# A decoder layer: pool history fetched in the head, pool products moved back, gate columns in fp32, output scaled in pieces

## The chip, the core and the metric

The kernel runs on one core of a Trainium2 chip. The metric is the device time of one execution in microseconds (us). TensorE (PE) multiplies matrices, VectorE (DVE) and ScalarE (ACT) do elementwise work, GpSimd (POOL) does a little elementwise work and issues DMAs, SyncE (SP) only issues DMAs.

## What is computed

One layer of a decoder trunk for 256 prompt tokens and 8 x 8 sample tokens: T = 320 token columns, model width 2048. All tensors are fp32.

```python
mod = silu(c) @ w_ada + b_ada                       # per sequence: sh1 sc1 g1 sh2 sc2 g2
h = rmsnorm(x, norm1_g) * (1 + sc1) + sh1
q, k, v, og, u, ga, gb, alr = split(h @ w_in)       # alr: 16 columns, the gate columns
loga = log_sigmoid(alr @ w_a2 + b_a) / 16
o, s_new = gla(q / 16, k, v, loga, state_gla)       # 4 heads, dk 256, dv 512
y_a = rmsnorm(o, gla_norm_g) * silu(og)
u_ext = concat(state_pool, u)                       # 15 history rows, then the new rows
y_b = (window_mean(u_ext, (2, 4, 8, 16)[g]) - u) @ w_pool[g] * pool_scale
x = x + g1 * ((sigmoid(ga) * y_a + sigmoid(gb) * y_b) @ w_o)
x = x + g2 * (swiglu(rmsnorm(x, norm2_g) * (1 + sc2) + sh2))
y = rmsnorm(x, final_norm_g)                        # also out: new GLA states, last 15 rows of u
```

## The kernel before

Activations lie transposed: features on 128 partitions, 320 tokens along the free axis. A product with a weight is done in three fp32r products (`mm3`): the weight and the activation are each split into a high part (a cast on ACT, `whi`, L157) and a low rest (a subtraction on DVE, `wlo`, L158), and high x high, high x low and low x high are summed in PSUM. Weights come through SP's queue into `raw` tiles of 512 KB; `whi` and `wlo` have four buffers each. A unit of 256 output columns over all 2048 inputs is 96 products into one tile `ps` of the PSUM pool `pmain`, which has two buffers. A unit's result is moved out by ACT or DVE, and only then is its buffer free.

The stages. The head (up to about 250 us) computes `mod` and h slice by slice, and with each slice of h the part that it adds to all units of group 0 (`SLICES`); 4 groups are the 4 heads with their pooling group. In the last slice, behind q's part, `alr_proj` makes the gate columns. Then groups 1 to 3 run: units q, k, v (two), u, og, ga, gb. While group h multiplies, the steps of group h - 1 (`gla_steps`, `pool_steps`, `merge_step`) are taken from a list `queue` ten at a time (`pump`), and a scheduler places all instructions on the engines by its own estimate of times. On the chip each engine then runs its instructions in that order. The tiles q, k, v and u have one buffer for all groups, so q of group 1 can leave PSUM only when the steps of group 0 have read q of group 0. The steps of the gates: `s_gk` (alr times w_a2, L591, then absolute value, exponential and logarithm, L599 to L606), `s_exp` (products with cumulative-sum matrices, L617 and L618, then exponentials, L622 to L627), `s_prod` (products with q and k, L633 to L653, among them kdA, a tile of the w4 buffers, L653), transposes, state products with S (L786, L807), and outputs. `pool_steps`: load history (`s_sp`), put it ahead of u (`s_hist`), write the new history (`s_buf`), window differences (`s_win`, giving dh and dl), and the products with w_pool (`s_y`, tiles `psy`, two PSUM buffers at once). The scaling of w_ada (`ada_burst`, L301) is done in fp32 with 32 columns of weights, four such products side by side in column tiles of TensorE.

After that come w_o, the feed-forward part and, at the end, the final norm: for each block k of 128 features the residual, its square, a transpose into token rows `yn` (L1093 to L1099), then the row sums (L1107), the scale `rr`, and the scaled rows stored through SP (L1119 to L1123).

Of the kernel before, what the change touches and what calls it, by code (L numbers as in the profile page):

```python
# [79 lines left out]
def body(tc, A):  # L80
# [759 lines left out]
    def pool_steps(g):  # L840
        h = g.h
        E = {}
        st = []
        u = g.u

        def s_sp():
            E["sp"] = lp.tile([NB * PB, 256], F32, tag="sp", name=nm("sp"))
            nc.gpsimd.dma_start(E["sp"], A["state_pool"][0, :, :, 256 * h:256 * h + 256].rearrange("b r c -> (b r) c"))
        st.append(s_sp)

        def s_hist():
            G.memset(u[:, :, 0:PB], 0.0)
            _, us = u_parts(g)
            pt = misc()
            for f in range(2):
                tr(pt[:, f * P:f * P + NB * PB], E["sp"][:, f * P:(f + 1) * P])
            for f in range(2):
                V.tensor_copy(us[:, f, :, 0:PB], pt[:, f * P:f * P + NB * PB].rearrange("p (b r) -> p b r", r=PB))
        st.append(s_hist)

        def s_buf():
            _, us = u_parts(g)
            cmt = w4([P, 2, P])
            G.memset(cmt[:, :, TS + PB:], 0.0)
            for f in range(2):
                G.tensor_copy(s3(cmt[:, f, 0:TS]), us[:, f, :, PB:])
                G.tensor_copy(cmt[:, f, TS:TS + PB], u[:, f, UEP - PB:UEP])
            pt = misc()
            for f in range(2):
                tr(pt[:, f * P:(f + 1) * P], cmt[:, f])  # L870
            t = lp.tile([P, DV], F32, tag="sf", name=nm("nb"))[:, 0:256]
            V.tensor_copy(t, pt[:, 0:256])
            for b in range(NB):
                nc.gpsimd.dma_start(A["o_ps"][0, b, PB - LS:PB, 256 * h:256 * h + 256], t[8 * b:8 * b + 8])
            nc.gpsimd.dma_start(A["o_pp"][0, 0, :, 256 * h:256 * h + 256], t[TS:TS + PB])
        st.append(s_buf)

        def s_win():
            cur = u
            ws = 1  # L880
            n = 0
            while ws < WINDOWS[h]:
                t = w4([P, 2, UEW])
                V.tensor_tensor(t[:, :, ws:], cur[:, :, ws:], cur[:, :, 0:UEW - ws], op=ALU.add)
                if 2 * ws < WINDOWS[h]:
                    V.tensor_copy(t[:, :, 0:ws], cur[:, :, 0:ws])
                cur = t
                ws *= 2
            w = WINDOWS[h]
            d = w4([P, 2, T])  # L890
            up, us = u_parts(g)
            cp_, cs = cur[:, :, PB:UEP], cur[:, :, UEP:UEW].rearrange("p f (b t) -> p f b t", t=PB + LS)
            V.scalar_tensor_tensor(d[:, :, 0:TP], cp_, 1.0 / w, up, op0=ALU.mult, op1=ALU.subtract)
            for f in range(2):
                V.scalar_tensor_tensor(s3(d[:, f, TP:T]), cs[:, f, :, PB:], 1.0 / w, us[:, f, :, PB:],
                                       op0=ALU.mult, op1=ALU.subtract)
                V.tensor_tensor(d[:, f, 0:16], cp_[:, f, 0:16], invc[:, 16 * h:16 * h + 16], op=ALU.mult)
                V.tensor_tensor(d[:, f, 0:16], d[:, f, 0:16], up[:, f, 0:16], op=ALU.subtract)
            dh = lp.tile([P, 2, T], F32R, tag="dh", name=nm("dh"))
            dl = lp.tile([P, 2, T], F32R, tag="dl", name=nm("dl"))  # L900
            hilo(dh, dl, d)
            E["dh"], E["dl"] = dh, dl
        st.append(s_win)

        def s_y():
            pp = [pmain.tile([P, 2, 512], F32, tag="pm", name=nm("psy")) for _ in range(2)]
            for k, whi, wlo in split_chunk(A["w_pool"][0, h].rearrange("(k p) n -> p k n", p=P), 2, 512):
                for e in range(4):
                    mm3(pp[e // 2][:, e % 2, :T], whi[:, e * P:(e + 1) * P], wlo[:, e * P:(e + 1) * P],
                        E["dh"][:, k], E["dl"][:, k], k == 0, k == 1)  # L910
            for i, ps in enumerate(pp):
                for e in range(2):
                    ee = 2 * i + e
                    V.scalar_tensor_tensor(g.gb[:, ee], ps[:, e, 0:T], PSC[:, 4 * h + ee:4 * h + ee + 1], g.gb[:, ee],
                                           op0=ALU.mult, op1=ALU.mult)
        return st, [s_y]

# [135 lines left out]
    for pi, (f0, f1) in enumerate(parts):  # L1053
# [24 lines left out]
        else:  # L1078
# [4 lines left out]
            for xg in xgs:  # L1083
                G.memset(xg[:, T:3 * P], 0.0)
        for ui in range(8):
            ps = proj(wdn, 256 * ui, f0, f1, ah, al)
            for i in range(2):
                k = 2 * ui + i
                residual(ps, i, k, 5)
                if pi == 1:  # L1090
# [2 lines left out]
                    S.activation(xg[:, 0:T], x1[k], AF.Copy, scale=FG[:, k:k + 1])  # L1093
                    pt = misc()
                    for a in range(3):
                        tr(pt[:, a * P:(a + 1) * P], xg[:, a * P:(a + 1) * P])
                    for a in range(3):
                        n = P if a < 2 else TS
                        (S.copy if a == 0 else V.tensor_copy)(yn[a][:n, k * P:(k + 1) * P], pt[:n, a * P:(a + 1) * P])  # L1099
# [14 lines left out]
    for a in range(3):  # L1114
        n = P if a < 2 else TS
        for c in range(2):
            sl = yn[a][:n, c * 1024:(c + 1) * 1024]
            if c == 0:
                V.tensor_scalar(sl, sl, rr[:n, 2 * a:2 * a + 1], None, op0=ALU.mult)  # L1119
            else:  # L1120
                S.activation(sl, sl, AF.Copy, scale=rr[:n, 2 * a:2 * a + 1])
            dst = A["y_p"][0, a * P:(a + 1) * P] if a < 2 else ys
            nc.sync.dma_start(dst[:, c * 1024:(c + 1) * 1024], sl)  # L1123
# [22 lines left out]
```

## Time and profile before

| | |
|---|---|
| median of 3 runs | 1978.41 us (1978.18 to 1979.74) |
| the profiled execution | 1972.99 us, its span 1971.2 us |
| TensorE busy | 1924.5 us, 98% |
| VectorE, ScalarE, GpSimd busy | 1007.0, 826.9, 207.3 us |
| DMA | 400.60 MB, mean 203 GB/s |
| granted TensorE clock, mean | 0.993 of full |

A row of the timeline gives the start, the time from the first start to the last end of a run of like instructions, the engine, the line of the kernel, the operation, the tiles out<-in, their shapes and how many; in brackets stands how long the engine stood idle ahead of it and what it waited for. Two TensorE instructions overlap, so the step from one start to the next is what one costs. PEld is the weight load, which runs beside the products. The granted clock is 1.00 at full speed and 0.50 at half.

### The profile page before, as it was taken

The page shows a single profiled execution, that of the slowest core. Times are in us where ns is not written, and L with a number is a line of the kernel's source. Part 1 is how long each engine was busy: PE and PEld are TensorE (multiplying, and loading weights), DVE is VectorE, ACT ScalarE, POOL GpSimd, SP SyncE. Part 2 cuts the span into 40 slices and gives each one's busy share as a digit, 9 for nine tenths or more (in the row PEclk, how much of TensorE's full clock was granted, in tenths as well). Part 3 has the DMA queues.
Part 4 walks back from the last instruction along what each step waited for, and adds up shares of the span by engine and source line. Part 5 has one row for each costly group of instructions (what it writes and reads, how often), then busy time and mean ns, then how long its engine had stood idle before and what let it go on. Part 6 is the DMA issues. An engine that isn't in the chain of part 4 may idle for free.

```text
span 1971.2 us, 34613 instructions
## 1 busy us (share of the span) xinstructions
PE 1924.5 (98%) x13808; PEld 1825.2 (93%) x13808; DVE 1007.0 (51%) x1935; ACT 826.9 (42%) x1485; POOL 207.3 (11%) x323
## 2 busy tenths in 40 slices
PE   5999999999999999999999999999999999999997
PEld 4889888988998899989989999999999999999997
DVE  3776454666355535665574444444444444444554
ACT  4433343544345433553354333333333434344443
POOL 2231131221121112111030000000000000000000
PEclk9999989999999999999999999999999999999998
DMA  9996647777875788579845555444545444444442
GB/s 349 354 354 237 203 150 264 219 230 251 256 223 188 247 268 272 183 249 321 269 153 158 186 188 182 145 150 144 156 145 155 150 150 150 150 151 144 149 139 98
DMA packets 287308, 400.60 MB, mean 203 GB/s; under 512 B 11953, under 2 KB 243921, under 8 KB 286809
## 3 DMA queue, kind: packets, MB, share of 16 engines
q1 hardware_dynamic: 250170, 261.81, 42.7%
q0 software_dynamic: 36976, 136.57, 19.5%
q8 instruction: 108, 1.77, 0.4%
q14 instruction: 54, 0.44, 0.1%
HBM read 373.90 MB, written 24.67 MB: 202 GB/s over the span
## 4 chain that ended last, share of the span: by engine, by line
PE 82%; DMA 3%; ACT 1%; DVE 0%; issue 0%; POOL 0%; ACTq 0%; DVEq 0%
PE ps L172 25%; PE ps L171 25%; PE ps L173 25%; PE pm L301 3%; PE pm L135 1%; DMA araw<-w_ada 1%; PE pm L786 1%; PE pm L807 1%; DMA raw<-w_o 1%; DMA S<-state_gla 1%; PE pm L752 1%; DMA o_gs<-S 0%; PE pm L782 0%; PE pm L591 0%; PE pm L741 0%; PE psy L171 0%
## 5 line engine op out<-in xcount | busy, mean ns | idle before, releaser
L158 DVE TENSOR_TENSOR wlo<-raw,whi 128x512 fp32r<-128x512 f32 x952 | 657.7, 694 | 792.4 <-ACT whi L157 779.9
L157 ACT CAST whi<-raw 128x512 fp32r<-128x512 f32 x952 | 587.8, 622 | 948.3 <-PE ps L172 830.1
L171 PE MATMUL ps<-hh,whi 128*128 128x320 f32 x1408 | 441.9, 314 | 6.1 <-ACT hh L337 2.6
L172 PE MATMUL ps<-hl,whi 128*128 128x320 f32 x1408 | 440.4, 313 | 0.0
L173 PE MATMUL ps<-hh,wlo 128*128 128x320 f32 x1408 | 437.4, 312 | 0.0
L172 PE MATMUL ps<-h2l,whi 128*128 128x320 f32 x1408 | 434.7, 309 | 0.0
L171 PE MATMUL ps<-h2h,whi 128*128 128x320 f32 x1408 | 434.7, 309 | 0.0
L173 PE MATMUL ps<-h2h,wlo 128*128 128x320 f32 x1408 | 434.2, 309 | 0.0
L171 PEld LDWEIGHTS ps<-hh,whi 128*128 128x128 f32 x1408 | 265.2, 188 | 19.7 <-issue 9.0
L172 PEld LDWEIGHTS ps<-hl,whi 128*128 128x128 f32 x1408 | 265.3, 188 | 10.4 <-issue 9.4
L173 PEld LDWEIGHTS ps<-hh,wlo 128*128 128x128 f32 x1408 | 264.7, 188 | 8.0 <-issue 5.3
L171 PEld LDWEIGHTS ps<-h2h,whi 128*128 128x128 f32 x1408 | 264.4, 188 | 3.4 <-ACT ah L337 3.4
L172 PEld LDWEIGHTS ps<-h2l,whi 128*128 128x128 f32 x1408 | 264.5, 188 | 0.1
L173 PEld LDWEIGHTS ps<-h2h,wlo 128*128 128x128 f32 x1408 | 264.5, 188 | 0.0
L171 PE MATMUL ps<-ah,whi 128*128 128x320 f32 x704 | 217.7, 309 | 0.0
L172 PE MATMUL ps<-al,whi 128*128 128x320 f32 x704 | 216.5, 308 | 0.0
L173 PE MATMUL ps<-ah,wlo 128*128 128x320 f32 x704 | 216.5, 308 | 0.0
L172 PEld LDWEIGHTS ps<-al,whi 128*128 128x128 f32 x704 | 132.0, 187 | 0.0
L171 PEld LDWEIGHTS ps<-ah,whi 128*128 128x128 f32 x704 | 131.9, 187 | 0.0
L173 PEld LDWEIGHTS ps<-ah,wlo 128*128 128x128 f32 x704 | 131.9, 187 | 0.0
L269 POOL DMA_DIRECT2D araw<-w_ada x64 | 55.1, 864 | 397.2 <-PE pm L301 385.9
L172 PE MATMUL ps<-ml,whi 128*128 128x320 f32 x256 | 79.3, 310 | 0.0
(282 smaller groups left out, 1634.2 us busy)
## 6 DMA issues: line engine op xcount, KB each, us to landing
raw<-w_gu SPq DMA_DIRECT2D x176, 512.0 KB, 3.5
raw<-w_in SPq DMA_DIRECT2D x170, 512.0 KB, 4.4
araw<-w_ada POOLq DMA_DIRECT2D x64, 1024.0 KB, 8.7
raw<-w_down SPq DMA_DIRECT2D x80, 512.0 KB, 3.5
hraw<-w_ada POOLq DMA_DIRECT2D x28, 1024.0 KB, 9.8
S<-state_gla POOLq DMA_DIRECT2D x16, 1024.0 KB, 8.3
o_gs<-S POOLq DMA_DIRECT2D x16, 1024.0 KB, 6.9
raw<-w_o SPq DMA_DIRECT2D x32, 512.0 KB, 6.2
```

What stands on the lines that cost most here:

```text
L135: PE.transpose(out, in_, ident[:k, :k])
L157: S.copy(hi, raw)
L158: V.tensor_sub(lo, raw, hi.bitcast(F32))
L171: PE.matmul(ps, lhsT=whi, rhs=xhi, start=start, stop=False)
L172: PE.matmul(ps, lhsT=whi, rhs=xlo, start=False, stop=False)
L173: last_mm[:] = [PE.matmul(ps, lhsT=wlo, rhs=xhi, start=False, stop=stop).ins]
L269: nc.gpsimd.dma_start(t[:, r:r + step], wada[:, k0 + r:k0 + r + step, col:col + nb * P])
L301: PE.matmul(ps[32 * j:32 * j + 32, 0:w], lhsT=scT[:, k0 + r + j, :], rhs=ada_raw[n][:, r + j, :], start=k0 == 0 and first, stop=k0 + nk == ...
L752: PE.matmul(pt, lhsT=E["kdn"][:, s, d * P:(d + 1) * P], rhs=E["vn"][:, s], start=s == 0, stop=s == 1)
L786: PE.matmul(pt[32 * j:32 * j + 32, :], lhsT=qeP[:, d, 4 * gg + j, :], rhs=E["S0", gg, d][:, j], start=False, stop=d == 0, tile_position=(0 ...
L807: PE.matmul(pt, lhsT=E["kpn"][:, j, d * P:(d + 1) * P], rhs=E["vp"][:, gg], start=True, stop=True)
```

## The change

Four things are done.

- The gate columns: `alr_proj` no longer splits the 16 columns of w_in into high and low parts in `wal` tiles. It multiplies the fp32 columns (`walr`, padded to 32) with hh and with hl, both read as fp32, in four column tiles; each tile sums a quarter of the input blocks. The four partial sums lie in four strips of 32 rows of alr, and w_a2 is loaded four times, one copy for each strip, so that `s_gk` adds them up.
- Group 0's pool history: `s_sp` and `s_hist` of group 0 are called in the head, behind `alr_proj`; `pool_steps` is moved ahead of the head in the file, and the tile sp comes from another pool.
- Group 0's pool products: `s_y` is put behind all GLA steps of group 0 in the list, where it stood behind the twelfth.
- The output: rows are scaled and stored in three pieces of 896, 896 and 256 columns in place of two of 1024, rows 0 to 127 and the sample rows by DVE, rows 128 to 255 by ACT; blocks 14 and 15 are turned into rows behind the first piece.

```diff
         def alr_proj(walr, cum):
             V.tensor_copy(cumr, cum)
             pa = misc()
-            for k0 in range(0, KT, 8):
-                wal = []
-                for tag in ("whi", "wlo"):
-                    t = wp.tile([P, 8, 64], F32R, tag=tag, bufs=WB, name=nm("wal"))
-                    G.memset(t.bitcast(F32), 0.0)
-                    wal.append(t)
-                wk = walr[:, k0:k0 + 8]
-                S.copy(wal[0][:, :, 0:16], wk)
-                V.tensor_sub(wal[1][:, :, 0:16], wk, wal[0][:, :, 0:16].bitcast(F32))
-                for j in range(8):
-                    k = k0 + j
-                    mm3(pa[:64, 0:T], wal[0][:, j], wal[1][:, j], hh[k], hl[k], k == 0, k == KT - 1)
+            with tc.high_priority(), tc.issue_after(last_mm[0]):
+                for r in range(0, KT, 4):
+                    for n, x in enumerate((hh, hl)):
+                        for j in range(4):
+                            PE.matmul(pa[32 * j:32 * j + 32, 0:T], lhsT=walr[:, r + j, :], rhs=x[r + j].bitcast(F32),
+                                      start=r + n == 0, stop=r == KT - 4 and n == 1, tile_position=(0, 32 * j))
             G.memset(alr, 0.0)
-            G.memset(alr[32:33, :], 1.0)
-            V.tensor_copy(alr[0:16, 0:T], pa[0:16, 0:T])
+            G.memset(alr[0:32, :], 1.0)
+            for j in range(4):
+                V.tensor_copy(alr[32 * j:32 * j + 16, 0:T], pa[32 * j:32 * j + 16, 0:T])
...
+                if last and ui == 0:
+                    pst, psy = pool_steps(g0)
+                    pst.pop(0)()
+                    pst.pop(0)()
...
-            nc.gpsimd.dma_start(wa2[0:16, :], A["w_a2"][0, :, DK * h:DK * h + DK])
-            nc.gpsimd.dma_start(wa2[32:33, :], A["b_a"][:, DK * h:DK * h + DK])
+            for j in range(4):
+                nc.gpsimd.dma_start(wa2[32 * j:32 * j + 16, :], A["w_a2"][0, :, DK * h:DK * h + DK])
+            nc.gpsimd.dma_start(wa2[16:17, :], A["b_a"][:, DK * h:DK * h + DK])
...
-    pst, psy = pool_steps(g0)
...
-    queue += pst + st[:PSY] + [sig0] + psy + st[PSY:] + [merge_step(g0, E)]
+    queue += pst + st[:PSY] + [sig0] + st[PSY:] + psy + [merge_step(g0, E)]
...
                 if pi == 1:
                     sq_acc(acc2, k, k == 0)
-                    xg = xgs[k % 2]
...
+                    if ui < 7:
+                        to_rows(k)
...
+    for a, eng in ((0, V), (1, S), (2, V)):
+        finish(a, 0, 896, eng)
+    for k in (14, 15):
+        to_rows(k)
+    for a, eng in ((0, V), (1, S), (2, V)):
+        finish(a, 896, 1792, eng)
+    for a, eng in ((0, V), (1, S), (2, V)):
+        finish(a, 1792, D, eng)
```

(`to_rows` holds the transposes that stood in the loop; `finish` scales and stores columns c0 to c1 of a block of rows.)

How the instructions move. TensorE, behind q's part in the last slice of the head (ps_2123 and ps_2124 are that part, wal and walr the gate columns), before:

```order
L173 MATMUL ps_2046<-hh_97,wlo_2100 128x320
L171 MATMUL pm_2160<-hh_86,wal_2161 64x320
L172 MATMUL pm_2160<-hl_102,wal_2161 64x320
L171 MATMUL ps_2123<-hh_98,whi_2126 128x320
...
L171 MATMUL pm_2160<-hh_101,wal_2191 64x320
L172 MATMUL pm_2160<-hl_117,wal_2191 64x320
L173 MATMUL pm_2160<-hh_101,wal_2193 64x320
```

and now:

```order
L173 MATMUL ps_2124<-hh_101,wlo_2144 128x320
L582 MATMUL pm_2161<-hh_86,walr 32x320
L582 MATMUL pm_2161<-hh_87,walr 32x320
...
L582 MATMUL pm_2161<-hl_116,walr 32x320
L582 MATMUL pm_2161<-hl_117,walr 32x320
L135 MATMUL pm_2203<-cst,sp_2200 128x120 x2
L171 MATMUL ps_2211<-hh_98,whi_2214 128x320
```

48 instructions became 32, and the two transposes of the pool history (sp) stand behind them now, some 350 instructions sooner than before.

TensorE from the end of group 1's q (ps_2821) over its k (ps_3112) to its v (ps_3368), before; psy are group 0's pool products, L591, L617 and L618 the gates, vTP, w and EX transposes, of which w is kdA:

```order
L173 MATMUL ps_2821<-hh_101,wlo_2943 128x320
L171 MATMUL psy_3051<-dh_2746,whi_3055 128x320
...
L173 MATMUL psy_3052<-dh_2746,wlo_3072 128x320
L591 MATMUL pm_2762<-w_447_2758,alr 128x256 x2
L591 MATMUL pm_2763<-w_447_2758,alr 128x256
L171 MATMUL ps_3112<-hh_86,whi_3115 128x320
...
L617 MATMUL pm_2783<-cumr,w_452_2769 128x272
...
L135 MATMUL pm_3007<-cst,vTP 128x128 x4
L172 MATMUL ps_3112<-hl_117,whi_3233 128x320
L173 MATMUL ps_3112<-hh_101,wlo_3234 128x320
L135 MATMUL pm_3013<-cst,w_487_2978 128x128
...
L171 MATMUL ps_3368<-hh_86,whi_3371 128x320
```

and now, where q is ps_2837, k ps_3070 and v ps_3337, and 54 of k's 96 products stand ahead of L674, 42 behind it:

```order
L173 MATMUL ps_2837<-hh_101,wlo_2959 128x320
L171 MATMUL ps_3070<-hh_86,whi_3073 128x320
...
L674 MATMUL pm_2741<-w_443_2734,alr 128x256 x2
...
L173 MATMUL ps_3070<-hh_101,wlo_3192 128x320
L700 MATMUL pm_2762<-cumr,w_448_2748 128x272
...
L701 MATMUL pm_2780<-cumr,w_449_2749 128x400
L135 MATMUL pm_2980<-cst,vTP 128x128 x4
L135 MATMUL pm_2986<-cst,vTP 128x128 x4
L135 MATMUL pm_2992<-cst,w_457_2811 128x128
...
L171 MATMUL ps_3337<-hh_86,whi_3340 128x320
```

The pool products are gone from here (they stand behind v), and the last product of k now stands ahead of the cumulative products (L700), where 31 of k's products stood behind their first before.

ScalarE at the very end, before (x_14 and x_15 are the last two blocks):

```order
L986 ACTIVATE sq_20691<-x_15_9634 128x320
L1093 ACTIVATE xg_18948<-x_15_9634,vec 128x320
L1099 COPY yn_18944<-pm_20680 128x128
L1099 COPY yn_18944<-pm_20695 128x128
L1111 ACTIVATE rr<-pm_20702,epst 128x2 x2
L1111 ACTIVATE rr<-pm_20702,epst 64x2
L1121 ACTIVATE yn_18944<-yn_18944,rr 128x1024
```

and now:

```order
L990 ACTIVATE sq_20671<-x_15_9622 128x320
L1093 ACTIVATE xg_18936<-x_15_9622,vec 128x320
L1121 ACTIVATE rr<-pm_20674,epst 128x2 x2
L1121 ACTIVATE rr<-pm_20674,epst 64x2
L1131 ACTIVATE yn_18933<-yn_18933,rr 128x896
L1099 COPY yn_18932<-pm_20692 128x128
L1131 ACTIVATE yn_18933<-yn_18933,rr 128x896
```

The scale and the first piece come ahead of the copies of the last two blocks; on TensorE the row sums (L1117, before L1107) stand ahead of their transposes likewise.

More of the change, by code (lines that the diff above doesn't have):

```diff
@@ L420, in units, with w4, pool_steps, s_sp @@
                 ("gb", 0, OGB + DV * h), ("gb", 1, OGB + DV * h + 256)]
+    def w4(shape, dt=F32):
+        return lps[0].tile(shape, dt, tag="w4", bufs=4, name=nm("w4"))
+    lps = []
+    def pool_steps(g):
+        h = g.h
+        E = {}
+        st = []
+        u = g.u
+        def s_sp():
+            E["sp"] = gp.tile([NB * PB, 256], F32, tag="sp", name=nm("sp"))
+            nc.gpsimd.dma_start(E["sp"], A["state_pool"][0, :, :, 256 * h:256 * h + 256].rearrange("b r c -> (b r) c"))
+        st.append(s_sp)
+        def s_hist():
+            G.memset(u[:, :, 0:PB], 0.0)
+            _, us = u_parts(g)
+            pt = misc()
+            for f in range(2):
+                tr(pt[:, f * P:f * P + NB * PB], E["sp"][:, f * P:(f + 1) * P])
+            for f in range(2):
+                V.tensor_copy(us[:, f, :, 0:PB], pt[:, f * P:f * P + NB * PB].rearrange("p (b r) -> p b r", r=PB))
+        st.append(s_hist)
+        def s_buf():
+            _, us = u_parts(g)
+            cmt = w4([P, 2, P])
+            G.memset(cmt[:, :, TS + PB:], 0.0)
+            for f in range(2):
+                G.tensor_copy(s3(cmt[:, f, 0:TS]), us[:, f, :, PB:])
+                G.tensor_copy(cmt[:, f, TS:TS + PB], u[:, f, UEP - PB:UEP])
+            pt = misc()
+            for f in range(2):
+                tr(pt[:, f * P:(f + 1) * P], cmt[:, f])
+            t = lps[0].tile([P, DV], F32, tag="sf", name=nm("nb"))[:, 0:256]
+            V.tensor_copy(t, pt[:, 0:256])
+            for b in range(NB):
+                nc.gpsimd.dma_start(A["o_ps"][0, b, PB - LS:PB, 256 * h:256 * h + 256], t[8 * b:8 * b + 8])
+            nc.gpsimd.dma_start(A["o_pp"][0, 0, :, 256 * h:256 * h + 256], t[TS:TS + PB])
+        st.append(s_buf)
+        def s_win():
+            cur = u
+            ws = 1
+            n = 0
+            while ws < WINDOWS[h]:
+                t = w4([P, 2, UEW])
+                V.tensor_tensor(t[:, :, ws:], cur[:, :, ws:], cur[:, :, 0:UEW - ws], op=ALU.add)
+                if 2 * ws < WINDOWS[h]:
+                    V.tensor_copy(t[:, :, 0:ws], cur[:, :, 0:ws])
+                cur = t
+                ws *= 2
+            w = WINDOWS[h]
+            d = w4([P, 2, T])
+            up, us = u_parts(g)
+            cp_, cs = cur[:, :, PB:UEP], cur[:, :, UEP:UEW].rearrange("p f (b t) -> p f b t", t=PB + LS)
+            V.scalar_tensor_tensor(d[:, :, 0:TP], cp_, 1.0 / w, up, op0=ALU.mult, op1=ALU.subtract)
+            for f in range(2):
+                V.scalar_tensor_tensor(s3(d[:, f, TP:T]), cs[:, f, :, PB:], 1.0 / w, us[:, f, :, PB:],
+                                       op0=ALU.mult, op1=ALU.subtract)
+                V.tensor_tensor(d[:, f, 0:16], cp_[:, f, 0:16], invc[:, 16 * h:16 * h + 16], op=ALU.mult)
+                V.tensor_tensor(d[:, f, 0:16], d[:, f, 0:16], up[:, f, 0:16], op=ALU.subtract)
+            dh = lps[0].tile([P, 2, T], F32R, tag="dh", name=nm("dh"))
+            dl = lps[0].tile([P, 2, T], F32R, tag="dl", name=nm("dl"))
+            hilo(dh, dl, d)
+            E["dh"], E["dl"] = dh, dl
+        st.append(s_win)
+        def s_y():
+            pp = [pmain.tile([P, 2, 512], F32, tag="pm", name=nm("psy")) for _ in range(2)]
+            for k, whi, wlo in split_chunk(A["w_pool"][0, h].rearrange("(k p) n -> p k n", p=P), 2, 512):
+                for e in range(4):
+                    mm3(pp[e // 2][:, e % 2, :T], whi[:, e * P:(e + 1) * P], wlo[:, e * P:(e + 1) * P],
+                        E["dh"][:, k], E["dl"][:, k], k == 0, k == 1)
+            for i, ps in enumerate(pp):
+                for e in range(2):
+                    ee = 2 * i + e
+                    V.scalar_tensor_tensor(g.gb[:, ee], ps[:, e, 0:T], PSC[:, 4 * h + ee:4 * h + ee + 1], g.gb[:, ee],
+                                           op0=ALU.mult, op1=ALU.mult)
+        return st, [s_y]
@@ L518, in h_rows @@
                      lambda: (hada(1, b, raws.pop((1, b)), xp), h_post(b), h_post(b + 1))])
+        walr = xp.tile([P, KT, 32], F32, name="walr")
+        G.memset(walr, 0.0)
         for f in h_rows(0)[1::2]:
@@ L530, in body @@
                 with tc.issue_after(spilt[-1]):
-                    walr = xp.tile([P, KT, 16], F32, name="walr")
-                    nc.gpsimd.dma_start(walr, win[:, :, OAL:OAL + 16])
+                    nc.gpsimd.dma_start(walr[:, :, 0:16], win[:, :, OAL:OAL + 16])
                     nc.gpsimd.dma_start(msk, A["ci"])
@@ L562, in body @@
     lp = mix.enter_context(tc.tile_pool(name="lp", bufs=1))
+    lps.append(lp)
     qeP = lp.tile([P, 2, NB, 32], F32, name="qeP")
@@ L572, in body @@
     G.memset(attP, 0.0)
-    def w4(shape, dt=F32):
-        return lp.tile(shape, dt, tag="w4", bufs=4, name=nm("w4"))
     def gla_steps(g):
@@ L838, in gla_steps @@
         return st, E
[L840 to L916, printed above, removed]
@@ L1084, in body, with to_rows @@
                 G.memset(xg[:, T:3 * P], 0.0)
+            def to_rows(k):
+                xg = xgs[k % 2]
+                S.activation(xg[:, 0:T], x1[k], AF.Copy, scale=FG[:, k:k + 1])
+                pt = misc()
+                for a in range(3):
+                    tr(pt[:, a * P:(a + 1) * P], xg[:, a * P:(a + 1) * P])
+                for a in range(3):
+                    n = P if a < 2 else TS
+                    (S.copy if a == 0 else V.tensor_copy)(yn[a][:n, k * P:(k + 1) * P], pt[:n, a * P:(a + 1) * P])
         for ui in range(8):
@@ L1091, in body @@
                     sq_acc(acc2, k, k == 0)
-                    xg = xgs[k % 2]
[L1093 to L1099, printed above, removed]
+                    if ui < 7:
+                        to_rows(k)
             if pi == 1 and ui == 5:
@@ L1113, in body, with finish @@
     ys = A["y_s"].rearrange("b t d -> (b t) d")
-    for a in range(3):
+    def finish(a, c0, c1, eng):
         n = P if a < 2 else TS
[L1116 to L1123, printed above, removed]
+        sl = yn[a][:n, c0:c1]
+        if eng is V:
+            V.tensor_scalar(sl, sl, rr[:n, 2 * a:2 * a + 1], None, op0=ALU.mult)
+        else:
+            S.activation(sl, sl, AF.Copy, scale=rr[:n, 2 * a:2 * a + 1])
+        dst = A["y_p"][0, a * P:(a + 1) * P] if a < 2 else ys
+        nc.sync.dma_start(dst[:, c0:c1], sl)
+    for a, eng in ((0, V), (1, S), (2, V)):
[6 more added lines that the diff above has]
+        finish(a, 1792, D, eng)
     ctx.close()
```

## The prediction

> **What bounds the kernel now.** I read the page, then TensorE's timeline stretch by stretch, then the other engines where TensorE stood still.
>
> ```profile
> span 1971.2 us, 34613 instructions
> PE 1924.5 (98%) x13808; PEld 1825.2 (93%) x13808; DVE 1007.0 (51%) x1935; ACT 826.9 (42%) x1485; POOL 207.3 (11%) x323
> ```
>
> TensorE is the bound: busy for 1924.5 of 1971.2 us. Only three things can pay: TensorE work taken out, its idle time (46.7 us in all), and time at the lower clock. The change touches each once: the gate products (L171 to L173 on tile wal), the stretch from group 1's q to its v, and the tail.
>
> **Gate products.**
>
> ```profile
> 191.89 0.30 PE L171 MATMUL pm<-hh,wal 128*64 128x320 f32 x1
> ...
> 195.71 0.30 PE L173 MATMUL pm<-hh,wal 128*64 128x320 f32 x1
> ...
> 202.46 0.31 PE L171 MATMUL ps<-hh,whi 128*128 128x320 f32 x1
> ...
> 209.35 0.31 PE L173 MATMUL ps<-hh,wlo 128*128 128x320 f32 x1
> ...
> 209.59 1.93 PE L301 MATMUL pm<-araw,scT 128*32 128x256 f32 x32
> 211.71 0.31 PE L172 MATMUL ps<-hl,whi 128*128 128x320 f32 x1
> ```
>
> Matmuls overlap, so the price is the step from start to start: 2 of the 48 products on wal stand at 191.89, the other 46 run from 195.71 to 202.46, 0.147 us each. All 48 cost 7.05 us. The new form is that of L301: fp32, 32 columns, four tiles side by side. There 16 instructions (32 records) over 256 columns took from 209.35 to 211.71, less two ordinary steps of 0.147, or 2.07 us, of which about 0.2 is for going in and out. 32 instructions over 320 columns: 2 x 1.25 x 1.87 + 0.2 = 4.9 us. Term: -2.2. Bounds: -2.4 (nothing for going in and out) and -1.9 (paid twice). The two casts, two subtractions and four fills of wal stood beside matmuls, so they give nothing. Three more copies into alr on DVE cost nothing: 48 matmuls of k and u (7 us) follow with their weights already split.
>
> **From q to v of group 1.** Here the pool products leave.
>
> ```profile
> 261.73 0.31 PE L173 MATMUL ps<-hh,wlo 128*128 128x320 f32 x1
> 264.46 0.63 PE L171 MATMUL psy<-dh,whi 128*128 128x320 f32 x1 [2.42 <-ACT dh L337]
> ...
> 269.72 0.64 PE L171 MATMUL psy<-dh,whi 128*128 128x320 f32 x1 [1.10 <-DVE mg L914]
> 270.15 0.47 PE L172 MATMUL psy<-dl,whi 128*128 128x320 f32 x1
> ...
> 273.09 2.09 PE L591 MATMUL pm<-w,alr 128*128 128x256 f32 x6
> ...
> 286.48 0.51 PE L618 MATMUL pm<-cumr,w 128*128 128x128 f32 x2
> ...
> 290.49 1.03 PE L135 MATMUL pm<-cst,vTP 128*128 128x128 f32 x8
> ...
> 292.14 0.30 PE L135 MATMUL pm<-cst,w 128*128 128x128 f32 x1 [0.33 <-DVE w L653]
> 293.20 0.39 PE L171 MATMUL ps<-hh,whi 128*128 128x320 f32 x1
> ```
> ```profile
> 25.19:28.60 3.41, 1.58 (x32) 0.81 (x23) 1.66 (x3) 2.12 (x4) 1.93 (x3) 1.00 1.04 403
> 260.70:264.11 3.41, 1.34 (x10) 1.07 (x8) 2.90 (x10) 1.13 (x3) 2.63 (x6) 1.00 1.05 367
> 264.11:274.35 10.24, 8.56 (x27) 7.56 (x28) 3.55 (x7) 1.53 (x3) 2.87 (x7) 0.50 0.38 108
> ```
>
> (In the second fence: stretch, length, busy time of PE, PEld, DVE, ACT and POOL, granted clock, DMA share, GB/s.) q ends, the pool products wait 2.42 us for dh, the clock falls to 0.50 for 10.24 us, and 24 products take until 273.09. Only then come the gates' second product (L591), k's 96 products and v: 293.20 - 261.73 = 31.47 us. v cannot start sooner than q of group 0 has been read: v's PSUM buffer is q's, and q is written to SBUF only then. That chain now becomes the bound, since in the new order k's 96 products are used up before it ends: 54 before L591, 42 behind it.
>
> ```profile
> 386.97 1.29 PE pm L591 x6
> 387.87 0.87 ACT L599 ACTIVATE w<-pm 128x512 f32<-128x512 f32 x2 [0.54 <-PE pm L591]
> 274.84 0.87 ACT L599 ACTIVATE w<-pm 128x512 f32<-128x512 f32 x2 [1.10 <-PE pm L591]
> 277.02 0.85 ACT L601 ACTIVATE w<-w 128x768 f32<-128x768 f32 x1
> 277.78 0.60 ACT L157 CAST whi<-raw 128x512 fp32r<-128x512 f32 x1
> 278.29 0.93 ACT L602 ACTIVATE w<-w,onet 128x768 f32<-128x768 f32 x1
> 279.25 1.02 DVE L604 SCALAR_TENSOR_TENSOR w<-pm,w 128x512 f32<-128x512 f32 x2
> 280.88 0.83 ACT L605 CAST w<-w 128x768 fp32r<-128x768 f32 x1
> 281.80 0.96 DVE L606 TENSOR_TENSOR w<-w,w 128x768 fp32r<-128x768 f32 x1
> 285.77 0.28 PE L618 MATMUL pm<-cumr,w 128*128 128x272 f32 x1
> 286.27 0.28 ACT L622 ACTIVATE EQK<-pm 128x128 f32<-128x128 f32 x1 [1.73 <-PE pm L618]
> 291.12 0.68 DVE L158 TENSOR_TENSOR wlo<-raw,whi 128x512 fp32r<-128x512 f32 x1
> 291.72 0.47 DVE L653 TENSOR_SCALAR w<-EX 128x128 f32<-128x128 f32 x2
> ```
>
> Counted from the start of L599: 3.03 to the end of L601, two weight casts between (one before) at 0.51 each, L602 0.93, L604 1.02, L605 0.83, L606 0.96: 7.8 us. Then 0.5 from L618 to the first exponential, and from 286.27 to L653 at 291.12 (the split ahead of it is gone from that place) 4.85, 0.42 to TensorE, 1.06 to v, and 0.13 for the pair of transposes that now stands ahead of v: 14.8 in all. Ahead of it 0.15 for q's last product, 54 x 0.147 = 7.94, and 0.90 from L591 to L599 (386.97 to 387.87, at full clock). New stretch: 23.8 us. Term: -7.7. Bounds: -8.7, if the two casts cost nothing, and -6.2, with the 1.5 us that DVE's other weight work and L605's delay (280.27 to 280.88) could add.
>
> The rest of this place is paid back. **The 24 products** stand behind v now: 24 x 0.147 = 3.5, and 0.3 because their second PSUM buffer is v's, which ACT empties after two copies: +3.8 (from 3.5 to 4.9, the latter with a wait of 1.10 again plus a 0.3). dh is long ready there. **The clock**: after L606 (7.8 on the count above) TensorE has the last cumulative products, 1.2 us (285.77 to 286.99), and vTP's transposes, 0.8 (290.49 to 291.28, where a product of k follows now), and then nothing until kdA at 7.8 + 0.5 + 4.85 + 0.42 = 13.6: idle for 3.8 us in one piece. A stretch of 3.41 us that was busy for 1.34 was followed by half clock, one busy for 1.58 was not: idle of about 2 us in such a stretch is enough, and 3.8 us reach it in nearly every position. At half clock a product takes 0.267 (11 from 270.15 to 273.09) for 0.147, a loss of 0.45 us per us. Bounds: 0, and 4.1 if half clock lasts 10.24 us again, 1.2 of it within the idle. I take one to two stretches, +1.8, because nothing waits behind v as the second psy half did at 269.72. The Trainium skill, page "TensorE: Matmul & The Clock Gate", section "Part 1: The HAM clock gate", gives the same free-running window of 3413 ns and lets the clock back after one busy window; by that alone the price would be 3.41 x 0.45 = 1.5. The 10.24 us above, three windows, show that a broken window does not count as busy, so I stay above it.
>
> **S and the queues.** Group 0's second S reload follows its o_gs store.
>
> ```profile
> 319.77 0.77 POOL L811 DMA_DIRECT2D o_gs<-S  x1 [3.37 <-DVE S L809]
> 336.78 1.92 PE L786 MATMUL pm<-S,qeP 128*32 128x512 f32 x16 [0.56 <-DMA S<-state_gla]
> ```
>
> From store to use 17.0 us. In the new order 71 products of ps and psy (10.4 us) and the attention products, which I put at another 10, stand between the last update of S and that use: some 3 us of slack. But two araw loads of 1 MB now enter POOL's queue between the first store and the reload, 5 us of all DMA engines at the 400 GB/s of the tail's rows below. 0, from -0.6 (the wait gone) to +3. Three more w_a2 issues per group (0.5 each on POOL, POOL 11% busy) are ahead of L591 by 8 us in group 0 and about 1 us in group 1: 0, up to +1. On SP's queue w_pool's load moves back past w_in loads of k and v, and its products stand some 40 us later than they did: 0. Group 0's state_pool load moves into the head, where DMA share is 0.95 to 1.00: 0.12 MB at 350 GB/s is 0.3: +0.3 (0 to 0.5).
>
> **Tail.**
>
> ```profile
> 1957.52 0.49 DVE L987 TENSOR_TENSOR acc<-acc,sq 128x320 f32<-128x320 f32 x1 [0.32 <-ACT sq L986]
> 1958.48 1.28 PEld L1107 LDWEIGHTS pm<-cst,acc 128*128 128x128 f32 x6
> 1961.22 2.90 SPq L1123 DMA_DIRECT2D y_p<-yn  x4
> 1962.00:1967.00 5.00, 0.00 (x0) 0.00 (x0) 0.53 (x1) 1.61 (x2) 0.00 (x0) 0.50 1.01 400
> 1968.00:1969.00 1.00, 0.00 (x0) 0.00 (x0) 0.00 (x0) 0.00 (x0) 0.00 (x0) 0.50 1.03 213
> ```
>
> acc is ready at 1958.01, but L1107's loads stand behind six transposes until 1958.48: now 0.45 sooner, and so is the first store, a little more with a piece an eighth shorter: 0.5. Behind that the DMA engines bound the end (share 1.01); y_s, from 64 partitions, runs at 213 GB/s. If mixing y_s with y_p filled the other half, its 0.52 MB would take 1.3 us in place of 2.5: -1.7. I take -1.0, bounds -2.0 and 0 (nine issues for six). The Trainium skill, page "SBUF — State Buffer", section "Door 1: The DMA port swizzle", says that partitions 0 to 63 reach only 8 of 16 ports; 213 against 400 GB/s agrees. By it a change of order alone gives no more than the start, -0.5.
>
> **Sum**: -2.2 - 7.7 + 3.8 + 1.8 + 0 + 0.3 - 1.0 = -5.0 us on a profiled time of 1972.99 (span 1971.2 and 1.8 around it). The median of the runs is 1978.41, 5.4 above that execution; I subtract there: 1973.4.
>
> **Rivals.** (1) The wait only moves. The half clock lasts three stretches again (+2.3) and the chain takes 1.5 us longer: -1.2, 1977.2. For it: the chain holds ACT, DVE and TensorE in turn, with no product left to fill. Against: k's products now run at full clock. Chance 0.28. (2) All of it pays: no fall of the clock and mixed stores, -5.0 - 1.8 - 1.0 = -7.8, 1970.6; needs the idle split by a stretch's border almost evenly, or a quicker chain. Chance 0.15. (3) Slower: the four column tiles run one after another. 32 instructions on fp32 then cost 4 x 4.7 = 18.8 us for 7.05, +14 on my -2.2: +9, 1987. It decides once the 32 take over 16 us. Against: L301's 16 instructions of the same kind in 2.07 us; for: those read other operands (scT, araw), and no row shows hh and hl read as fp32. Chance 0.05. The forecast has 0.52, with a range of its own from -3 to -7 us.
>
> **Numbers.** 0.2% (4 us) is about what can be told from no change. Faster: three quarters of the forecast, all of (2), some of (1): 0.56. Same: the rest of these, 0.37. Slower: 0.07, (3) and a late S on top of (1). Range 1969.6 to 1977.6: from (2) with the larger tail bound to (1) with 0.4 us more; outside remain (3) and the ends of the others.
>
> **What would show it.** The gate products take 4.9 us on TensorE; no wait at psy; a new idle of 3 to 4 us ahead of the first v product of group 1, named after DVE's kdA (w), with half clock behind it; psy behind v at 0.147 a product; first store 0.5 us sooner after the last ps product. Wrong it would be if L700's first product waits for more than 2 us, if the clock stays at 1.00 there, or if TensorE waits over 2 us for S.

## The result: slower by 0.5%, and the time is lost far from the edit

| | before | after |
|---|---|---|
| median (runs beside each other) | 1977.45 us | 1986.49 us (1979.93 to 1989.81) |
| ratio | | 1.0054, 95% interval 1.0040 to 1.0069 |
| profiled execution, its span | 1972.99, 1971.2 us | 1989.72, 1987.9 us |

The prediction was 1973.4 us. The medians stand 9.0 us apart, the profiled executions 16.7, since before's was one of its quickest and after's one of its slowest; the account below is of those two, and the experiments give the medians.

The page of the changed kernel, span and busy time:

```profile
span 1987.9 us, 34669 instructions
PE 1928.4 (97%) x13824; PEld 1821.3 (92%) x13824; DVE 1009.9 (51%) x1939; ACT 818.5 (41%) x1479; POOL 209.8 (11%) x332
```

TensorE is busy 4 us longer, although it has less to do, and idle 13 us longer. Where, is seen from instructions that occur once per unit, such as the one that moves a unit's result out of PSUM. Of before, the timeline of ACT and DVE (start, duration), q of groups 2 and 3, w_o's first unit and its fifth:

```profile
495.58 0.70 ACT L397 ACTIVATE q<-ps 128x640 f32<-128x640 f32 x1
696.81 0.70 ACT L397 ACTIVATE q<-ps 128x640 f32<-128x640 f32 x1
900.62 0.48 DVE L991 SCALAR_TENSOR_TENSOR x<-ps,mod,x 128x256 f32<-128x256 f32 x1
960.39 0.48 DVE L991 SCALAR_TENSOR_TENSOR x<-ps,mod,x 128x256 f32<-128x256 f32 x1
```

and of after:

```profile
498.89 0.70 ACT L397 ACTIVATE q<-ps 128x640 f32<-128x640 f32 x1
701.82 0.70 ACT L397 ACTIVATE q<-ps 128x640 f32<-128x640 f32 x1
905.01 0.47 DVE L995 SCALAR_TENSOR_TENSOR x<-ps,mod,x 128x256 f32<-128x256 f32 x1
976.76 0.47 DVE L995 SCALAR_TENSOR_TENSOR x<-ps,mod,x 128x256 f32<-128x256 f32 x1
```

After lags by 3.3, 5.0, 4.4 and then 16.4 us: 12 of the 16.7 us go in 60 us of the w_o stage, where the diff changes no line. Before is the quickest there of all kernels below with the full bytes: from w_o's first unit to its fifth the profiled executions of before, e2 to e6, e9, e11 and e12 take 59.8 to 64.7 us, those of after, e1 and e7 69.5 to 71.8. So 12 is the upper end of a loss of 5 to 12 us. Stretches of the trace (stretch, length, busy PE, PEld, DVE, ACT, POOL, granted clock, DMA share, GB/s), before and then after:

```profile
845.00:880.00 35.00, 35.00 (x274) 30.62 (x273) 24.92 (x52) 20.23 (x39) 4.38 (x6) 1.00 0.70 233
880.00:940.00 60.00, 58.66 (x436) 55.91 (x435) 32.56 (x70) 23.74 (x44) 10.59 (x16) 1.00 0.96 320
```
```profile
845.00:880.00 35.00, 35.00 (x234) 29.55 (x227) 18.95 (x41) 18.28 (x37) 4.78 (x7) 1.00 0.65 223
880.00:940.00 60.00, 53.57 (x414) 47.77 (x417) 30.29 (x65) 20.24 (x39) 10.27 (x15) 0.97 1.02 344
```

In w_o's first 60 us the DMA engines are full (1.02, 0.96 before), TensorE stands idle for 6.4 us and half clock follows (0.97). From 870 to 1000 us TensorE waits 5.0 us for whi and wlo, which are made from w_o's weights, 1.9 for adasb (0.9 before, 2.2 in e9, whose araw loads come in time) and 1.8 for mg, the mixed rows that w_o multiplies (no such wait before). What the DMA engines carry is seen on POOL's queue. Before, group 3 from its w_a2 load on (w_a is w_a2; araw are the columns of w_ada for the scaling products of L301; the tick is a copy of one column of og, which holds the next araw load back until og is there):

```profile
776.25 0.51 POOL L585 DMA_DIRECT2D w<-w_a  x1 [0.29 <-POOL w L584]
...
780.73 0.19 POOL L275 COPY tick<-og 128x1 f32<-128x1 f32 x1 [3.48 <-DVE og L411]
781.25 1.84 POOL L269 DMA_DIRECT2D araw<-w_ada  x2 [0.33 <-issue]
...
824.90 0.81 POOL L811 DMA_DIRECT2D o_gs<-S  x1 [8.41 <-DVE S L809]
...
861.47 0.76 POOL L811 DMA_DIRECT2D o_gs<-S  x1 [3.71 <-DVE S L809]
865.03 1.79 POOL L269 DMA_DIRECT2D araw<-w_ada  x2 [2.80 <-PE pm L301]
```

and after:

```profile
786.25 0.19 POOL L275 COPY tick<-og 128x1 f32<-128x1 f32 x1 [4.03 <-DVE w L485]
786.81 1.81 POOL L269 DMA_DIRECT2D araw<-w_ada  x2 [0.38 <-issue]
788.61 1.99 POOL L668 DMA_DIRECT2D w<-w_a  x4
...
840.52 0.85 POOL L894 DMA_DIRECT2D o_gs<-S  x1 [3.16 <-DVE S L892]
...
881.94 0.76 POOL L894 DMA_DIRECT2D o_gs<-S  x1 [6.09 <-DVE S L892]
882.70 1.78 POOL L269 DMA_DIRECT2D araw<-w_ada  x2
```

The w_a2 loads, four now, stand behind og's tick and a pair of 1 MB araw loads, where the single one stood ahead. The scheduler put group 3's gate product some 70 products of TensorE later in the order (89.4 us behind group 3's q in before, 100.0 in after; e7 has the same 100 with nothing changed but the loads), the first state store comes 15.6 us later, the last 20.5, and the three araw pairs that stand behind the stores, 6 MB, leave POOL from 882.70 on instead of 865.03: no longer beside the end of group 3, where DMA had room, but beside w_o's weights. SP's rows show those weights: the tenth to thirteenth issue of w_o take 15.8 us before and 22.3 after:

```profile
904.88 15.75 SPq L149 DMA_DIRECT2D raw<-w_o  x4
```
```profile
909.27 22.29 SPq L149 DMA_DIRECT2D raw<-w_o  x4
```

### The profile page after: what moved, and what is told of

The parts are those of the page before. It is cut to its first block, busy times and chain, and to the rows that moved or that the text cites. A ratio compares the mean times of both kernels' runs of the same rounds, so it can differ in the third digit from the quotient of the medians.

```text
span 1987.9 us, 34669 instructions
## 1 busy us (share of the span) xinstructions
PE 1928.4 (97%) x13824; PEld 1821.3 (92%) x13824; DVE 1009.9 (51%) x1939; ACT 818.5 (41%) x1479; POOL 209.8 (11%) x332
## 4 chain that ended last, share of the span: by engine, by line
PE 89%; DMA 5%; DVE 2%; ACT 1%; SPq 1%; issue 1%; POOL 0%; DVEq 0%; ACTq 0%
PE ps L171 27%; PE ps L172 26%; PE ps L173 26%; PE pm L301 3%; PE pm L135 2%; DMA raw<-w_o 1%; DMA raw<-w_in 1%; DMA araw<-w_ada 1%; PE pm L236 1%; PE pm L869 1%; DMA o_gs<-S 1%; PE pm L890 1%; DVE wlo L158 1%; SPq L225 1%; PE pm L835 1%
## 5 line engine op out<-in xcount | busy, mean ns | idle before, releaser
L171 PE MATMUL ps<-hh,whi 128*128 128x320 f32 x1408 | 442.8, 315 | 7.2 <-ACT hh L337 2.6
L171 PE MATMUL ps<-h2h,whi 128*128 128x320 f32 x1408 | 434.6, 309 | 0.0
L171 PEld LDWEIGHTS ps<-hh,whi 128*128 128x128 f32 x1408 | 265.6, 189 | 25.7 <-issue 13.1
L171 PEld LDWEIGHTS ps<-h2h,whi 128*128 128x128 f32 x1408 | 264.3, 188 | 3.4 <-ACT ah L337 3.4
L171 PE MATMUL ps<-ah,whi 128*128 128x320 f32 x704 | 217.7, 309 | 0.0
L171 PEld LDWEIGHTS ps<-ah,whi 128*128 128x128 f32 x704 | 131.9, 187 | 0.0
L171 PE MATMUL ps<-mh,whi 128*128 128x320 f32 x256 | 80.4, 314 | 5.2 <-ACT whi L157 3.4
```

The costliest lines, as they stand in the source:

```text
L171: PE.matmul(ps, lhsT=whi, rhs=xhi, start=start, stop=False)
```

## The experiments

Medians, with those of the kernel before run beside them on the same chip.

| run | median | before | ratio, 95% interval |
|---|---|---|---|
| e1, gate columns alone | 1989.26 | 1975.72 | 1.0068 (1.0054 to 1.0083) |
| e2, pool work alone | 1972.98 | 1975.72 | 0.9988 (0.9978 to 0.9998) |
| e3, output alone | 1978.62 | 1975.72 | 1.0012 (1.0002 to 1.0021) |
| e4, after with one w_a2 load | 1974.35 | 1975.72 | 0.9995 (0.9986 to 1.0005) |
| e5, e4 with before's output | 1972.16 | 1975.16 | 0.9988 (0.9978 to 0.9998) |
| e6, e4 with two pieces | 1972.55 | 1975.16 | 0.9988 (0.9977 to 0.9999) |
| e7, before with three idle loads | 1991.29 | 1975.16 | 1.0090 (1.0076 to 1.0104) |
| e8, after with less araw | 1975.94 | 1975.16 | 1.0009 (0.9999 to 1.0020) |
| e9, after with the loads on SP | 1971.86 | 1975.52 | 0.9980 (0.9969 to 0.9990) |
| e10, before with less araw | 1973.95 | 1975.52 | 0.9991 (0.9980 to 1.0001) |
| e11, e9 with before's output | 1970.92 | 1975.52 | 0.9979 (0.9970 to 0.9988) |
| e12, pool products alone | 1975.05 | 1975.52 | 1.0004 (0.9994 to 1.0014) |

The kernel before itself has medians from 1975.16 to 1977.45 in these comparisons, so differences of about 2 us between two rows with different values of before decide nothing.

Theory A is the one above: the loads of w_a2, through the order and POOL's queue. The others stand in the expectations.

**The three parts alone.** Each is the part of the diff by that name, put into the kernel before. e1, the gate columns:

> The kernel before with the gate columns alone changed (fp32 in column tiles, four loads of w_a2 per group). Theory A, the four loads of w_a2: they delay the gates of groups 2 and 3 in the scheduler's order (the gates' product of group 3 stands 70 products, 10 us, later), so the last state stores and the araw loads behind them on POOL's queue start some 17 us later and meet the w_o weights: the w_o stage loses 5 to 12 us, TensorE stands idle there, the gate products gain 1.4; in all +4 to +11 us against before. Rival B, the moved pool work is what costs: here it is not moved, so -1.4 us. Rival C, the loss in the w_o stage is an accident of single executions: -1.4 us at the median, with some executions 10 us longer.

+13.5 us, more than the whole change and more than A's upper end. The w_o stage is that of after; before, after and e1:

```profile
870.00:1000.00 130.00, 128.66 (x931) 124.79 (x930) 71.46 (x151) 54.13 (x98) 15.90 (x26) 1.00 0.84 278
870.00:1000.00 130.00, 121.34 (x870) 113.70 (x869) 71.31 (x152) 49.81 (x95) 19.72 (x28) 0.99 0.83 279
870.00:1000.00 130.00, 122.66 (x877) 114.81 (x876) 73.79 (x160) 51.98 (x101) 17.90 (x28) 0.99 0.83 277
```

Before is idle for 1.3 us, after for 8.7, e1 for 7.3. B and C fall.

e2, the pool work:

> The kernel before with group 0's pool history in the head and its pool products last, nothing else. Theory A: the w_o stage is that of before (no idle of TensorE there beyond 1 us), since the order of groups 2 and 3 is unchanged; the stretch from q to v of group 1 gains 8 to 9 us, 4 go back to the pool products behind v, 2 to a later reload of S, 2 to half clock: -2 us (-4 to +1). Rival B: +6 to +10 us, with the loss in the w_o stage. Rival C: -2 us at the median, single executions 10 us longer.

-2.7 us, within A's range. Between k and v of group 1 the clock stays at 1.00 here:

```profile
276.00:292.00 16.00, 12.54 (x88) 9.63 (x87) 10.61 (x29) 8.79 (x30) 3.98 (x6) 1.00 0.65 201
```

and between 250 and 360 us TensorE waits nowhere for S. So this part does what was predicted of it, and its w_o stage shows no loss (60.5 us from the first unit to the fifth).

e3, the output:

> The kernel before with the output in three pieces alone. Theories A, B and C: 0 us (-1 to +1), since in the changed kernel the end of the last product to the end of the span was 16.5 us against 16.3 before. The prediction had -1.0.

+2.9 us. SP's stores, whose last product of TensorE starts at 1959.81:

```profile
1966.00 1.51 SPq L1129 DMA_DIRECT2D y_p<-yn  x3
...
1973.30 0.47 SPq L1129 DMA_DIRECT2D y_s<-yn  x1
```

The first store leaves 6.19 us after the last product, 6.66 before (1954.56 to 1961.22), but the ninth is issued 14.0 us after it, where the sixth was at 12.2 (1964.17 + 2.54); from the last product to the end it is 17.3 us for 16.6. That is 0.7 of the 2.9. Over all profiled executions the five with nine stores take 16.5 to 17.3 us for it (e3, e4, e8, e9, after), the eight with the output as before 15.9 to 16.9, so even the 0.7 is little more than executions differ. The diff leaves everything ahead of the output as it was, so the rest is not explained by these profiles; e9 against e11, with and without the three pieces, differ by 0.9.

**The loads.** e4 keeps the column tiles but adds up the four strips on TensorE:

```diff
+ sel: 128 x 32, four unit matrices below each other
+ V.tensor_copy(st4, pa[:, 0:T]); PE.matmul(pb[0:32, 0:T], lhsT=sel, rhs=st4)
- for j in range(4): load w_a2 into wa2[32 * j:32 * j + 16]
+ load w_a2 into wa2[0:16]
```

> The changed kernel whole, but the four partial sums of the gate columns are added by one TensorE product with a 128 x 32 selection matrix in the head, and w_a2 is loaded once per group as before. The order of groups 2 and 3 is then that of before. Theory A: the loss of the w_o stage is gone; against before -2 us (-5 to +1). Rival B: as the changed kernel, +6 to +10 us. Rival C: -2 us at the median, single executions 10 us longer; then the changed kernel's median would have to be a matter of chance too.

-1.4 us (its interval includes no change), and the order of groups 2 and 3 is that of before again. B falls here too. e7 is the reverse: nothing of the change, only the loads.

```diff
  load w_a2 into wa2[0:16]
+ for r in (48, 64, 96): load w_a2 into wa2[r:r + 16]
```

> The kernel before with nothing changed but three more loads of w_a2 per group, into rows of the tile that are multiplied by zero rows of alr. Theory A, the loads alone are the cause: the gates of group 3 move back by 70 products in the order, the last araw loads by some 15 us, the w_o stage loses 8 to 11 us: +11 us against before (+8 to +14). Rival D, the new form of the gate columns on TensorE, DVE and POOL is the cause: 0 us (-1 to +2).

+16.1 us, above the range that A gave. POOL's queue in group 3 is that of after (one load of w_a2 and three more behind og's araw pair):

```profile
790.09 1.80 POOL L269 DMA_DIRECT2D araw<-w_ada  x2 [0.38 <-issue]
791.89 0.53 POOL L585 DMA_DIRECT2D w<-w_a  x1
...
792.91 1.43 POOL L588 DMA_DIRECT2D w<-w_a  x3
...
885.96 1.78 POOL L269 DMA_DIRECT2D araw<-w_ada  x2 [0.21 <-issue]
```

By the units, its lag grows from 2.0 us after the head, where nothing is changed, to 7.6 at w_o's first unit and 18.2 at its fifth: 10.5 in the w_o stage and 5.6 in groups 1 to 3. One wait of the 5.6 is named: v of group 1 waits 2.9 us for q to leave PSUM (`PE ps L171 <- ACT q L397`), which it does not in before. So the loads alone are enough: A holds, D falls, and the groups themselves pay too, which A had not priced.

e9 leaves the four loads and moves them to SP's queue (`nc.sync.dma_start`):

> The changed kernel whole, with its four loads of w_a2 per group (the load of b_a stays on POOL), but these four issued on SP's queue in place of POOL's. The order of groups 2 and 3 is then within a few products of that of before. Theory A, refined: it is where the loads stand on POOL's queue, ahead of and behind the araw loads and the state stores, and the later gates that follow from it; then -1.4 us against before as with one load (-4 to +1), with under 4 us of TensorE idle between 870 and 1000. Rival G, the four loads themselves cost wherever they stand: +7 to +11 us. Rival H, on SP's queue they hold up the weights behind them: TensorE waits for whi or raw in groups 1 to 3, 0 to +6 us.

-3.7 us. POOL's rows show the araw loads back in their place:

```profile
777.32 1.85 POOL L269 DMA_DIRECT2D araw<-w_ada  x2 [0.36 <-issue]
...
821.54 0.81 POOL L894 DMA_DIRECT2D o_gs<-S  x1 [9.20 <-DVE S L892]
...
862.35 1.78 POOL L269 DMA_DIRECT2D araw<-w_ada  x2 [2.62 <-PE pm L301]
```

The same loads with the same bytes cost nearly 13 us more on POOL's queue (+9.0 for after) than on SP's: G falls, and H with it: between 360 and 900 us TensorE's waits add up to 0.2 us. The move to SP changes the place of the loads on the queue and the scheduler's order together, so no run tells how much is due to each.

**Bytes or order in the w_o stage?** e8 leaves 6 MB out of the changed kernel, e10 the same out of before (`LESS` are bursts 22 to 25; a burst of them reads its half tile twice):

```diff
- ada_want.extend((n, t, r) for r in range(0, nk, ...))
+ ada_want.extend((n, t, r) for r in range(0, nk // 2 if n in LESS else nk, ...))
```

> The changed kernel, in which the last four scaling products of the mixing and w_o stages (bursts 22 to 25) load only half their columns of inputs (6 MB left out) and use that half twice; all other work is the same. Theory A, the w_o stage loses because too many bytes meet there: TensorE's idle time between 880 and 980 us falls from 9 us to under 2, and against before the kernel is at 0 us (-2 to +3). Rival F, it is the order of instructions on TensorE and POOL that holds it up there, whatever the bytes: +8 to +11 us as the changed kernel.

> Control to the run with less araw: the kernel before, with the same 6 MB of the last four scaling products left out. Theory A: the w_o stage of before is short of few bytes only, so -1 us (-3 to 0), and the gain of 10 us from the same cut in the changed kernel is the collision. Rival F (order, not bytes): the cut gives 0 here, and gave nothing there either. Rival I, leaving 6 MB out saves much in any kernel: -6 us or more.

+0.8 us against before for e8, -1.6 for e10 (both intervals include no change). Of the 9 us by which after was slower, 8 go with the bytes, and the same cut is worth 1.6 where the araw loads come in time, so by these medians some 6.6 are due to the bytes coming late. The loads as a whole cost 10.4 us (after against e4) to 12.7 (against e9), so some 4 to 6 us of their cost are not taken away by leaving these bytes out. I, a saving of 6 us or more in any kernel, falls. e8's stretch:

```profile
870.00:1000.00 130.00, 128.20 (x946) 123.13 (x945) 75.93 (x159) 54.19 (x98) 13.30 (x24) 1.00 0.75 246
```

Idle 1.8 us for 8.7, DMA share 0.75 for 0.83. The gate product stands as late as in after; only the bytes are fewer. What is left of the idle is the wait of 1.8 us for mg. So F falls for the larger part: in the w_o stage the late order does most of its harm through the DMA engines, and the wait for mg, with what groups 1 to 3 lose, stays.

**What is left to gain.** e5 is e4, e11 is e9, both with the output as before; e6 is e4 with the row sums ahead of the last transposes and two pieces of 1024.

> The kernel before with group 0's pool work moved and with the gate columns in fp32 column tiles, the four partial sums added by one TensorE product, w_a2 loaded once per group; the output as before. Theory A: the moved pool work gives its -2.7 us, the gate columns another -1.4, the sum's product takes back 0.3: -3.8 us against before (-6 to -2). Rival D, the fp32 column tiles cost elsewhere what they save: -2.7 us or less gain. Rival E, any change in front of the w_o stage upsets it: 0 or slower.

> The same with the row sums ahead of the last two blocks' transposes, but two pieces of 1024 columns, six stores in place of nine. If the three-piece output lost by its three additional stores on SP's queue, the first store is 0.5 us sooner after the last product and the end too: -4.3 us against before. If it lost because the last rows are turned so late, the end comes 0 to 0.5 us later than in the run beside it: -3.5 us.

> As the run with the loads on SP's queue, but the output as before. Theory A with the tail's loss of 1 to 2 us taken out: -3 us against before (-5 to -1), no slower than the version with one load and a sum. Rival H: 0 to +5 us.

e5 -3.0, e6 -2.6, e11 -4.6 us. e11 beats both kernels (its interval is clear of no change). E falls. e5 against e2 (-2.7) leaves for the gate columns 0.3 us, e11 against e2 1.9, neither of which can be told from none here, so D is not decided for e5. In e6 the end comes 16.3 us after the last product, as in e11 (16.3), with six stores: it neither gains nor loses, and neither of its two forecasts came. The additional stores are the likelier reason for e3's 0.7 (the last of nine is issued 13.2 to 14.0 us after the last product, the last of six 11.4 to 12.2), but that is argued, not shown.

e12, pool products moved, history where it was:

> The kernel before with group 0's pool products moved last and nothing else; the history stays where it was. If the gain of the moved pool work (-2.7 us) is all the products', -2.5 us (-4 to -1). If the history in the head is needed for it, since its transposes and loads now stand ahead of the gates of group 0, 0 us (-1 to +1), with a wait of TensorE between q and k of group 1.

No gain. TensorE's waits from 250 to 360 us:

```profile
PE pm L617 <- ACT w L605: 5.6, 1, 5.6
PE pm L135 <- DVE w L653: 2.3, 1, 2.3
```

With the history in its old place the order has the gate product behind all of k, so that nothing covers the chain of ACT and DVE, 5.6 us of waiting behind k (it was expected between q and k). So the products' move needs the history's move to pay; the history's move alone was not run.

## Why the prediction was wrong, step by step

**The step that failed** is in "S and the queues": "Three more w_a2 issues per group (0.5 each on POOL, POOL 11% busy) are ahead of L591 by 8 us in group 0 and about 1 us in group 1: 0, up to +1." It priced the loads by their issue time and looked at groups 0 and 1. After (+9.0) against e4 (-1.4) and e9 (-3.7), they cost 10 to 13 us, by the profiled executions 5 to 12 of them in the w_o stage and the rest in groups 1 to 3 (5.6 in e7). The issues do take 0.5 us each (1.99 for four); what they did was to push the gates of group 3 behind the next araw loads, and with them everything that POOL's queue holds behind the state stores (group 2's four still stand ahead of theirs). The order of group 3 was at hand and shows it; the prediction read the order only where the diff had moved something. Its list of what would make it wrong has no sign for a place behind group 1.

**Gate products: right on TensorE, worth less in the time.** Rows of after, the 32 products and what follows:

```profile
198.95 0.74 PE L582 MATMUL pm<-hh,walr 128*32 128x320 f32 x8
...
202.74 0.72 PE L582 MATMUL pm<-hl,walr 128*32 128x320 f32 x8
203.39 0.42 PE L135 MATMUL pm<-cst,sp 120*128 120x120 f32 x2
```

4.4 us, predicted 4.9, for 7.05: rival (3), tiles one after another, is out. But a new wait of 0.65 for whi appears just ahead of them, the transposes of the history stand behind them, and the lag shrinks there by 1.3, not 2.6. At the median the gate columns bring 0.3 (e5 against e2) to 1.9 (e11 against e2), for a term of 2.2.

**From q to v: size off by 1.6.** Rows of after, from q's last product to v's first (262.88 is k's first):

```profile
262.74 0.31 PE L173 MATMUL ps<-hh,wlo 128*128 128x320 f32 x1
...
270.80 1.46 PE L674 MATMUL pm<-w,alr 128*128 128x256 f32 x6
278.81 0.88 PE L700 MATMUL pm<-cumr,w 128*128 128x272 f32 x4 [0.38 <-ACT w L688]
...
282.00 1.09 PE L135 MATMUL pm<-cst,vTP 128*128 128x128 f32 x8 [0.82 <-ACT EX L709]
285.72 0.45 PE L135 MATMUL pm<-cst,w 128*128 128x128 f32 x1 [2.63 <-DVE w L736]
...
288.17 0.61 PE L171 MATMUL ps<-hh,whi 128*128 128x320 f32 x1
```

25.4 us, predicted 23.8, for 31.5. The chain is the one named, and its last wait is the one named (kdA, w), 2.6 us in place of 3.8, since a part of the idle stands ahead of vTP and L700. L700 did not wait long, psy not at all. The 31.5 are one execution's: e3, with before's order here, takes 28.3 us (263.65 to 291.94), since its clock stays at 1.00 from 260 to 275 us, where before has a mean of 0.66. A good part of the term of -7.7 was taken from a fall of the clock that not every execution has.

**The clock: as priced in after, and no fall in e2.** The stretch of e2 above, in after:

```profile
276.00:292.00 16.00, 12.00 (x70) 9.95 (x72) 11.89 (x33) 9.25 (x29) 3.98 (x6) 0.89 0.47 151
```

16 us at a mean of 0.89 are 3.5 us at half clock, one stretch. Predicted one to two, +1.8. The Trainium skill, page "TensorE: Matmul & The Clock Gate", section "Part 1: The HAM clock gate", lets the clock back after one busy window of 3413 ns, and this place agrees. In e2, with nearly the same idle (12.5 busy of 16, to 12.0), the clock stays at 1.00: the clock's part of rival (2) happened there. Whether e2's clock stays up in every execution is not known from one profile.

**S: the bad bound came true.** TensorE's waits in after, 250 to 360 us:

```profile
PE pm L869 <- DMA S<-state_gla: 2.3, 1, 2.3
```

The prediction gave 0 to +3 and called more than 2 us a sign against it. A stretch of half clock follows here too (0.93 from 320 to 344 us). The loads are not needed for this wait: e4, with one load, has it with 2.0 us and the same 0.93, e8, with the four loads on POOL, has 0.5, and e2, e6 and e9 have none. So the slack of 3 us is used up in some of the profiled executions and not in others.

**Head: another reason than the one priced.** The state_pool load was costed by its bytes, +0.3, beside the last slice. POOL's rows of after from the start of the kernel:

```profile
2.75 0.52 POOL L600 MEMSET walr<- 128x512 f32 x1
...
3.58 0.69 POOL L435 DMA_DIRECT2D sp<-state_pool  x1
...
4.41 0.32 POOL masks.py:199 TENSOR_SCALAR_AFFINE_SELECT cst<-cst 128x128 f32<-128x128 f32 x1
```

The fill of walr and the load's issue stand ahead of the unit matrix that every transpose needs; it started at 3.26 before. The first product of the head starts 1.35 us later in after (33.62), 0.6 in e2 (32.91), against 32.27; in e3, e7, e10 and e12, whose heads are before's, 0.1 to 0.4 later. Just ahead of the gate products after is 2.5 us behind before, but there e3 and e7 are 1.9 and 2.0 behind too, so what this costs in the time can't be told from how executions differ.

**Output: wrong by its sign.** Predicted -1.0, measured +2.9 alone (e3) and +0.9 in e9 against e11. The start is 0.47 us sooner in e3, as said (0.5), but no gain of mixing y_s with y_p is seen and nine issues take longer than six. Here the Trainium skill's rule, quoted against the mixing (page "SBUF — State Buffer", section "Door 1: The DMA port swizzle"), by which only the start would be gained, was nearer.

With the loads on SP's queue (e9), the change is at -3.7 us, and the sum of the other terms was -5.0. That they come so near is in part luck: the pool work's terms (-7.7, +3.8, +1.8, +0.3) add up to -1.8 and e2 has -2.7, while the gate columns brought less than their 2.2 and the output lost.

## What to carry to other kernels

An additional small DMA is not priced by its issue time. Where a scheduler places instructions by its own estimate of times, ask what the DMA's user will be placed behind, follow the queue it is on to the next large transfer, and go through every later repetition of the loop, not only the one that the diff touches. Here the loads that feed such a chain cost 10 to 13 us on the queue where large transfers wait for that chain in turn, and nothing that shows on the other (e9).

## What was not expected of the hardware

A stage whose DMA engines are nearly full anyway (0.96 in before) turns lateness into time: 6 MB whose first pair is issued 22 us ahead of w_o's first unit (after, e1, e7) in place of 33 to 35 (the nine others with the full bytes) cost 5 to 12 us in the w_o stage, while leaving the same 6 MB out of the punctual kernel saved 1.6 us at the median, which can't be told from none. Executions of one and the same kernel differ there as well: before and e3, whose order is identical up to the output, lie 4.9 us apart between w_o's first unit and its fifth (59.8 us from 900.09 to 959.87 in before, 64.7 from 900.75 to 965.46 in e3, by the rows of L991). Why e3 fell on the slower side at its median too stays open.
